# A two-layer hybrid trunk in split fp32: the first output projection in pairs by seven products, and changes at the start, in the last pair and in the final norm

## The chip, the cores and the metric

One core of one Trainium2 chip. The metric is the device time of one execution in microseconds, the median over the runs. Engines are named as in the profile: PE (TensorE), DVE (VectorE), ACT (ScalarE), POOL (GpSimd), SP (SyncE, which here only issues transfers).

## The reference

Two layers act on x, which has 512 tokens of 1024 channels, all in float32. Each layer does this:

```python
h = rmsnorm(x, norm_g[layer])
u = h @ w_in[layer]                       # q, k, v, z of three mixers, and merge gates ga, gb, gc
...
merged = (sigmoid(ga) * (ya @ w_br_a[layer]) + sigmoid(gb) * (yb @ w_br_b[layer])
          + sigmoid(gc) * (yc @ w_br_c[layer]))
x = x + merged @ w_out[layer]
```

ya is forgetting attention (4 heads), yb a dilated mixture (6 heads), yc sliding-window attention with sinks (6 query heads on 2 key heads), each times a SiLU gate. A final RMSNorm of x follows the second layer.

## The kernel before

All activations are held transposed: a tile has 128 channels on the partitions and the 512 tokens as its free size, so x is 8 such tiles, k = 0 to 7. PE's fast fp32 format keeps only part of a number, so every operand is split in a high half (fp32r) and a low half (the rest), and every product is made of three matmuls: high times high, high times low, low times high (mm3, L128 to L132). The half sums go to one bank of PSUM. Weights come in chunks of 128 x 512: wh is the high half, wl the low half. For most weights POOL issues the load of wh, ACT writes the negated high half to wl (L1146), and POOL issues a second load that accumulates the weights on top (L1147): wl is then the low half, without work of DVE. For the weights that load raw (layer 0's V, and the last projection, "plain") ACT casts the high half (L1140) and DVE or POOL subtracts (L1142).

A list of items, built once, sets the order of the work: each has a PE function with the weight chunks it takes, or is an evacuation without chunks. A loop at the end walks through it (from L1180 on): ahead of a step it loads and splits what that step takes, behind it loads up to RINGH = 10 chunks ahead and splits up to RING = 7 ahead. The order written so is then refined by the compiler's scheduler, except in a stretch that is put under a manual schedule, where it stays as written.

Per layer: the V projection (v_item L225: for each k, four token blocks of three 512-column matmuls, in four "att" banks that collect over k), attention, the mixers' gate projections, and the merge of 8 output rows M0 to M7. Six of the merge's steps are pairs (pair_steps L646): two rows' gate products are worked out by seven products of half size instead of eight, from sums and differences of quarters of the weights and of x (forms 0 to 6; the sums of x are made once by sums L598, in four places SH and SL: vb, PH and PL, P). The pair's results of 256 columns are combined by DVE from banks a, b and c (c11, c12, c22, c21), with ACT's help, and each row is then normed, gated and merged (norm, gate, merge). merge writes the high half MH by ACT and the low half ML by DVE; M6 and M7 come from the last pair (2, 6).

Behind layer 0's merge stands the first output projection (o_item L778): 8 outputs e, each of 24 matmuls of 512 columns over the 8 merged rows. DVE adds the residual (L789), the sum goes out to x1d, ACT and DVE split it into XH and XL of the second layer (split_x L149), and its square is summed by ACT and POOL (square_sum L162). Between the outputs stand the second layer's V items.

Behind layer 1's merge stands the last projection (last_item, last_projection L861): 16 steps of 24 matmuls of 256 columns, first the first half of the tokens for the 8 outputs, then the second half. From the last pair of layer 1 on a manual schedule holds. DVE adds the residual (L828), ACT squares (L834, L837) and scales (L842), DVE sums the squares (L839). The final norm takes the column sums by PE (rms_pe, L176), a root by ACT and DVE (rms_root), a transpose of the reciprocal to a row on all partitions (rbc_pe, L217), a copy of it by ACT (L848) and the products (store_half, L856 on POOL, L858 on DVE).

The start: g goes out on ACT's queue (L106), the tiles of x and V's first weights in turn on SP's; ten matmuls of zeros (L1156) keep PE busy until the first V item.

## Time and profile before

| what | value |
| --- | --- |
| median of 3 runs | 881.96 us (880.96 to 884.07) |
| profiled execution, its time | 880.83 us |
| its span in the profile | 879.1 us |
| mean granted clock of PE | 0.995 |
| busy: PE, DVE, ACT, POOL | 864.6, 569.0, 510.8, 441.9 us |
| moved by DMA | 163.83 MB |

The span is the time from the first to the last instruction that the profile holds; the execution's own time is somewhat longer. Busy times of engines overlap. In a row of the timeline the first number is the start from the span's beginning, the second the duration, both in us, then engine, line, operation, what it writes and reads, shapes and how many are grouped; in brackets the idle time ahead of it and what ended that. Matmuls are pipelined, so their durations overlap and the time that each takes is the distance from start to start.

### The profile page before, as it was taken

Reading aid. Unit: us, or ns where it says so; the run is one execution under the profiler, and the core shown is the slowest. Engines: PE = TensorE matmul, PEld = TensorE weight load, DVE = VectorE, ACT = ScalarE, POOL = GpSimd, SP = SyncE. Lnnn points to the kernel's source line nnn. Section 1 sums busy time; section 2 is a strip of 40 time slices with the busy share of each in tenths; the row PEclk is TensorE's granted clock in tenths of the full one; section 3 lists DMA queues with packets and bytes.
Section 4 is the critical chain, followed back from the end, with each engine's and each line's share of the span. In section 5 each row is a group of like instructions: output and inputs, shape, how many; then the busy total and the mean of one; then the engine's idle time right before and its main releaser. Section 6 shows DMA issues by size and latency. Waiting matters only on the chain.

```text
span 879.1 us, 14412 instructions
## 1 busy us (share of the span) xinstructions
PE 864.6 (98%) x4866; PEld 750.8 (85%) x4866; DVE 569.0 (65%) x1250; ACT 510.8 (58%) x1076; POOL 441.9 (50%) x570
## 2 busy tenths in 40 slices
PE   9999999999999999999999999999999999999995
PEld 6988888888888899997889888888888888999994
DVE  7546688577676768762123658876685867687643
ACT  7377566575656655554335856666465765556552
POOL 5354576665444254566664546667544444544211
PEclk9999999999999999999999999999999999999998
DMA  8697777978989899999997887788799897998423
GB/s 293 142 212 146 152 151 166 184 149 180 196 188 235 205 181 249 206 192 288 255 240 151 173 167 153 146 168 172 157 205 199 181 249 162 206 250 189 133 71 113
DMA packets 97082, 163.83 MB, mean 186 GB/s; under 512 B 12144, under 2 KB 26864, under 8 KB 97008
## 3 DMA queue, kind: packets, MB, share of 16 engines
q0 software_dynamic: 71424, 121.70, 68.9%
q1 hardware_dynamic: 25440, 41.20, 14.2%
q8 instruction: 38, 0.62, 0.3%
q14 instruction: 36, 0.29, 0.1%
q10 hardware_dynamic: 144, 0.01, 0.0%
HBM read 153.43 MB, written 4.19 MB: 179 GB/s over the span
## 4 chain that ended last, share of the span: by engine, by line
PE 75%; issue 8%; POOL 6%; DMA 6%; DVE 3%; ACT 1%; SPq 0%; POOLq 0%; DVEq 0%; ACTq 0%
PE mm L130 16%; PE mm L131 16%; PE mm L132 16%; PE att L130 4%; PE att L131 3%; PE att L132 3%; PE pv L549 3%; POOL wl L1147 3%; POOL wh L1117 3%; PE att L503 3%; PE att L439 2%; PE att L438 2%; DMA tmp<-in_xT_dram 2%; PE att L234 1%; PE att L235 1%
## 5 line engine op out<-in xcount | busy, mean ns | idle before, releaser
L1147 POOL DMA_DIRECT2D wl<-in_wpk_dram x248 | 224.0, 921 | 179.4 <-ACT wl L1146 147.9
L1117 POOL DMA_DIRECT2D wh<-in_wpk_dram x248 | 168.8, 685 | 176.1 <-PE mm L132 129.4
L1146 ACT ACTIVATE wl<-wh 128x512 fp32r<-128x512 f32 (+3 forms) x248 | 147.9, 601 | 139.8 <-PE mm L132 107.5
L130 PE MATMUL mm<-xh,wh 128*128 128x512 f32 x544 | 217.7, 400 | 0.0
L131 PE MATMUL mm<-xl,wh 128*128 128x512 f32 x544 | 214.6, 394 | 0.0
L132 PE MATMUL mm<-xh,wl 128*128 128x512 f32 x544 | 214.4, 394 | 0.0
L132 PEld LDWEIGHTS mm<-xh,wl 128*128 128x128 f32 x544 | 102.2, 188 | 24.0
L130 PEld LDWEIGHTS mm<-xh,wh 128*128 128x128 f32 x544 | 102.4, 188 | 22.1
L131 PEld LDWEIGHTS mm<-xl,wh 128*128 128x128 f32 x544 | 102.4, 188 | 22.0
L474 ACT ACTIVATE P<-P,ng 128x256 f32<-128x256 f32 (+3 forms) x128 | 67.0, 525 | 24.6 <-DVE ng L472 24.1
L529 DVE TENSOR_TENSOR PL<-att,PH 128x512 fp32r<-128x512 f32 (+2 forms) x84 | 46.1, 599 | 7.0 <-ACT PH L528 7.0
L130 PE MATMUL mm<-y,wh 128*128 128x512 f32 (+1 forms) x132 | 49.9, 378 | 0.2 <-ACT y L711 0.2
L131 PE MATMUL mm<-y,wh 128*128 128x512 f32 (+1 forms) x132 | 49.9, 378 | 0.0
L132 PE MATMUL mm<-y,wl 128*128 128x512 f32 (+1 forms) x124 | 47.5, 383 | 0.0
L130 PE MATMUL att<-xh,wh 128*128 128x256 f32 x144 | 40.6, 282 | 1.3 <-DVE tmp L740 1.3
L132 PE MATMUL att<-xh,wl 128*128 128x256 f32 x144 | 40.4, 281 | 0.0
L131 PE MATMUL att<-xl,wh 128*128 128x256 f32 x144 | 40.4, 281 | 0.0
L492 DVE TENSOR_SCALAR P<-P,den 128x256 f32<-128x256 f32 (+3 forms) x128 | 39.7, 376 | 1.0
L528 ACT CAST PH<-att 128x512 fp32r<-128x512 f32 (+2 forms) x84 | 38.7, 526 | 1.3 <-PE att L503 0.6
L439 PE MATMUL att<-qk,qk 128*128 128x256 f32 (+2 forms) x128 | 37.0, 308 | 0.0
L503 PE MATMUL att<-ident,P 128*128 128x128 f32 x284 | 36.2, 272 | 0.0
L438 PE MATMUL att<-qk,qk 128*128 128x256 f32 (+2 forms) x128 | 36.1, 308 | 0.0
(260 smaller groups left out, 2039.4 us busy)
## 6 DMA issues: line engine op xcount, KB each, us to landing
wh<-in_wpk_dram POOLq DMA_DIRECT2D x196, 256.0 KB, 4.6
wl<-in_wpk_dram POOLq DMA_DIRECT2D x196, 256.0 KB, 5.1
y<-in_wpk_dram SPq DMA_DIRECT2D x32, 256.0 KB, 5.4
qk<-in_wpk_dram SPq DMA_DIRECT2D x24, 256.0 KB, 5.3
wh<-in_wpk_dram POOLq DMA_DIRECT2D x32, 192.0 KB, 4.7
wl<-in_wpk_dram POOLq DMA_DIRECT2D x32, 192.0 KB, 4.5
tmp<-tmp SPq DMA_DIRECT2D x80, 64.0 KB, 3.8
mg<-in_xT_dram SPq DMA_DIRECT2D x8, 256.0 KB, 6.6
```

The lines of the kernel that those rows point to most:

```text
L130: nc.tensor.matmul(ps, wh, xh, start=first, stop=False, skip_group_check=part)
L131: nc.tensor.matmul(ps, wh, xl, start=False, stop=False, skip_group_check=part)
L132: nc.tensor.matmul(ps, wl, xh, start=False, stop=last, skip_group_check=part)
L438: nc.tensor.matmul(ps, q[:, qs], kh[:, a:a + n], start=True, stop=False)
L439: nc.tensor.matmul(ps, q2[:, qs], k2[:, a:a + n], start=False, stop=True)
L474: nc.scalar.activation(pb, pb, AF.Exp, bias=ng[:, i:i + 1], scale=-1.0, accum_out=den[:, i:i + 1])
L492: nc.vector.tensor_scalar(blks[i], blks[i], den[:, i:i + 1], None, op0=ALU.mult)
L503: nc.tensor.transpose(ps[:, c * P:(c + 1) * P], pt[:, src * P:(src + 1) * P], st["ident"])
L529: nc.vector.tensor_tensor(st["PL"][:, o:o + n], bk[:, :n], rd(hh), op=ALU.subtract)
L1117: nc.gpsimd.dma_start(hl[i][0][:, :w], ap)
L1146: nc.scalar.activation(lo[:, :w], rd(h[:, :w]), AF.Copy, scale=-1.0)
L1147: nc.gpsimd.dma_start(lo[:, :w], ap, accum_op=ALU.add)
```

## The change

It has four parts.

1. *First loads.* g goes out first on SP, V's first weights on ACT's queue, and ACT's table load stands behind it. There are 7 warm-up matmuls in place of 10.
2. *First output projection.* Outputs 0 and 1 stay as they are. Outputs (2, 3), (4, 5), (6, 7) are pairs by seven products of 12 matmuls with 256 columns (o_pair). Their sums of x are now sums of the merged rows (four_sums, for k = 0 to 3), in the same places as before. The pairs' weights load raw by SP's queue, 4 quarters of 256 KB each, and are cast by ACT and subtracted by DVE (L1217 differences, L1238 casts, L1240 low halves). The squares are summed by DVE. The order is output 0, 1, pair (2, 3), V0, V1, pair (4, 5), V2, V3, pair (6, 7), V4 to V7. V's low halves stand in the tiles va0 to va3, which are empty then, and take no place of the seven of wl.
3. *Last pair of layer 1 and last projection.* Weights are loaded and split one step later, behind the evacuations of the step. Of the low halves of the last projection's first chunks, four stay on POOL and four go to DVE.
4. *Final norm.* The column sums begin with a matmul of zeros and then take all of the accumulator's columns, the last squares last. The reciprocal row of the second half is written to two banks, one for DVE and one for ACT.

```diff
-    nc.scalar.dma_start(g_sb, gT)
+    nc.sync.dma_start(g_sb, gT)
...
-            eng = nc.vector if k == KT - 1 else nc.gpsimd
+            eng = nc.vector if k == KT - 1 else side
...
-        for n, tb in enumerate(tbs):
-            for j, a in enumerate(accs):
-                nc.tensor.matmul(ps[:, tb:tb + 1], st[a][:, n * P:(n + 1) * P], ones,
-                                 start=j == 0, stop=j == len(accs) - 1)
+        zero = st["PH"]
+        c = slice(tbs[0], tbs[-1] + 1)
+        nc.tensor.matmul(ps[:, c], zero[:, :P], zero[:, :len(tbs)], start=True, stop=False)
+        for j, a in enumerate(accs):
+            for n, tb in enumerate(tbs):
+                nc.tensor.matmul(ps[:, tb:tb + 1], st[a][:, n * P:(n + 1) * P], ones, start=False,
+                                 stop=j == len(accs) - 1 and n == len(tbs) - 1)
...
+    def four_sums(k, a, b):
+        u, v = tmp(), tmp()
+        nc.vector.tensor_tensor(u[:, T0], a[:, T1], b[:, T1], op=ALU.add)
+        nc.vector.tensor_tensor(u[:, T1], u[:, T0], a[:, T0], op=ALU.subtract)
+        nc.vector.tensor_tensor(v[:, T0], a[:, T0], a[:, T1], op=ALU.subtract)
+        nc.vector.tensor_tensor(v[:, T1], b[:, T0], u[:, T1], op=ALU.subtract)
+        h, lo = sum_places(k)
+        for n, w in ((0, u), (1, v)):
+            c = slice(n * S, n * S + S)
+            nc.scalar.copy(h[:, c], w)
+            nc.vector.tensor_tensor(lo[:, c], w, rd(h[:, c]), op=ALU.subtract)
+        st["SH", k], st["SL", k] = h, lo
...
+    def o_pair(l, e, bank, res, finish):
...
+        def add(u, tok, b, first):
+            def run():
+                if u not in x:
+                    x[u] = tmp()
+                other = st["xr", e + u] if first else x[u]
+                nc.vector.tensor_tensor(x[u][:, tok], d[b], other[:, tok], op=ALU.add)
+                if not first:
+                    finish(e + u, x[u], tok)
+            return urgent(run)
+
+        res(e)
+        prod("a", 0, M(0, T0))
+        do(add(0, T0, "a", True))
+        prod("c", 1, M(1, T0))
+        do(add(0, T0, "c", False))
+        prod("b", 2, sum_part(1))
+        do(add(1, T1, "b", True))
+        prod("a", 3, sum_part(2))
+        do(add(1, T0, "a", True))
+        prod("b", 4, sum_part(4))
+        do(add(1, T0, "b", False))
+        prod("a", 5, sum_part(3))
+        do(add(1, T1, "a", False), add(0, T1, "a", True))
+        prod("e", 6, M(1, T1))
+        do(add(0, T1, "e", False))
...
-            o_item(0)
-            for e in range(1, 8):
-                o_item(e)
-                v_item(1, e - 1)
-            v_item(1, 7)
+            first_projection()
...
+    def first_projection():
...
+        do(lambda: load_res(0), lambda: load_res(1), sums_m(0))
+        o_item(0)
+        do(sums_m(1))
+        o_item(1)
+        do(sums_m(2), sums_m(3))
+        o_pair(0, 2, mm_bank, res, finish)
+        v_item(1, 0)
+        v_item(1, 1)
+        o_pair(0, 4, mm_bank, res, finish)
+        v_item(1, 2)
+        v_item(1, 3)
+        o_pair(0, 6, mm_bank, res, finish)
+        for k in range(4, 8):
+            v_item(1, k)
...
-                eng = nc.gpsimd if key[:2] == LAST_O and key[3] == 0 else nc.vector
+                eng = nc.gpsimd if key[:2] == LAST_O and key[3] == 0 and key[2] > 3 else nc.vector
...
-    for _ in range(10):
+    for _ in range(7):
...
-                    nc.sync.dma_start(t[:, :w], ap)
+                    (nc.scalar if i == 0 else nc.sync).dma_start(t[:, :w], ap)
...
+        if key[:2] == ("v", 1):
+            return h, T([P, S], F32R, f"va{key[2] % 4}")
...
+            if key[:2] != ("v", 1):
+                if since is not None and sum(j >= since for j in ring) >= RING:
+                    return
+                ring.append(i)
...
-        nc.scalar.copy(rbc, st["rb"][:, :HT])
+        nc.scalar.copy(rbc, st[f"rb{hf}"][:, :HT])
...
         step(lambda _: rbc_pe(_, h1))
+        step(lambda _: rbc_pe(_, h1, "rb1", att_bank))
         do(lambda: store_half(1))
...
+        if later is not None:
+            load(later + RINGH)
+            split_to(later + RING)
+            later = None
...
-        load(pos + RINGH if n > 4 else pos + 8)
-        split_to(pos + RING)
+        if "late" in st:
+            later = pos
+        else:
+            load(pos + RINGH if n > 4 else pos + 8)
+            split_to(pos + RINGH, pos)
```

How the order of the instructions moves, at two places. The first is DVE in the first output projection, behind the evacuation of the output before. Before, for outputs 0 to 2 (tmp is the sum, xl its low half):

```order
L789 TENSOR_TENSOR tmp_4451<-mm_4421,sz_4417 128x512
L159 SCALAR_TENSOR_TENSOR xl_883_4457<-tmp_4451,g_61,xh_882_4456 128x512
L789 TENSOR_TENSOR tmp_4497<-mm_4462,sz_4419 128x512
L159 SCALAR_TENSOR_TENSOR xl_893_4503<-tmp_4497,g_61,xh_892_4502 128x512
L789 TENSOR_TENSOR tmp_4565<-mm_4535,sz_4453 128x512
L159 SCALAR_TENSOR_TENSOR xl_909_4571<-tmp_4565,g_61,xh_908_4570 128x512
```

After, around output 1's addition (L803; wl are weights' low halves, L610 to L613 the four sums of merged rows, PL their low halves):

```order
L1240 TENSOR_TENSOR wl_4518<-xh_862_4319,wh_4408 128x512
L803 TENSOR_TENSOR tmp_4521<-mm_4485,sz_4420 128x512
L1240 TENSOR_TENSOR wl_4582<-xl_861_4317,wh_4459 128x512
L1240 TENSOR_TENSOR wl_4586<-xl_863_4321,wh_4510 128x512
L159 SCALAR_TENSOR_TENSOR xl_904_4525<-tmp_4521,g_61,xh_903_4524 128x512
L170 TENSOR_TENSOR ys_4471<-ys_4471,tmp_4528 128x512
L610 TENSOR_TENSOR tmp_4531<-mg_2025,mg_2698 128x256
L612 TENSOR_TENSOR tmp_4532<-mg_2025 128x256
L611 TENSOR_TENSOR tmp_4531<-tmp_4531,mg_2025 128x256
L610 TENSOR_TENSOR tmp_4541<-mg_2345,mg_2981 128x256
L613 TENSOR_TENSOR tmp_4532<-mg_2698,tmp_4531 128x256
```

Where two additions and splits of x followed each other, weight splits, the sum of squares and the sums of the merged rows now stand between them; wl_4586 is the low half of form 6 of pair (2, 3).

The second place is ACT, at the end of the last pair of layer 1 and the start of the last projection. Before (L692 the gate, L711 the high half of a merged row, L1140 weight casts, L834 and L837 squares, L842 scaling):

```order
L692 ACTIVATE tmp_8811<-tmp_8811 128x256
L711 CAST y_1744_8894<-mg_7262 128x256
L1140 CAST wh_8933<-xl_1749_8931 128x512
L834 ACTIVATE ys_9032<-mg_9028 128x256
L842 ACTIVATE mg_9028<-mg_9028,gf_294 128x256
L1140 CAST wh_8952<-xl_1753_8950 128x512
L1140 CAST wh_8981<-xh_1759_8979 128x512
L837 ACTIVATE tmp_9074<-mg_9070 128x256
```

After (L709, L728, L1238, L915, L918 and L923 are the same steps):

```order
L709 ACTIVATE tmp_9041<-tmp_9041 128x256
L728 CAST y_1791_9125<-mg_7499 128x256
L1238 CAST wh_9152<-xl_1796_9150 128x512
L915 ACTIVATE ys_9262<-mg_9258 128x256
L923 ACTIVATE mg_9258<-mg_9258,gf_291 128x256
L1238 CAST wh_9173<-xl_1799_9171 128x512
L918 ACTIVATE tmp_9301<-mg_9297 128x256
L923 ACTIVATE mg_9297<-mg_9297,gf_291 128x256
```

The cast ahead of the first square was that of output 3's first chunk (wh_8933) and is now that of output 2's second (wh_9152): output 3's first chunk (wh_9173) stands behind the first square and scaling, its second behind the next ones. And DVE there, after (L763 is c21, L716 and L717 the merge, L729 the low half of a merged row, L909 the additions of the residual):

```order
L1240 TENSOR_TENSOR wl_9201<-xl_1793_9129,wh_9131 128x512
L763 TENSOR_TENSOR tmp_9041<-att_9026,rbc_5356 128x256
L716 SCALAR_TENSOR_TENSOR tmp_9041<-tmp_9041,mm_9112 128x256
L717 TENSOR_TENSOR mg_7499<-mg_7499,tmp_9041 128x256
L729 TENSOR_TENSOR y_1792_9126<-mg_7499,y_1791_9125 128x256
L1240 TENSOR_TENSOR wl_9226<-xl_1796_9150,wh_9152 128x512
L909 TENSOR_TENSOR mg_9258<-mm_9233,sz_9229 128x256
L1240 TENSOR_TENSOR wl_9269<-xl_1799_9171,wh_9173 128x512
L909 TENSOR_TENSOR mg_9297<-mm_9272,sz_9231 128x256
```

wl_9201 and wl_9226 are output 2's low halves: the first was POOL's, the second stood ahead of c21; now the second stands behind the merge.

## Rows read from the trace of the kernel before

**Rows 1.** The page, busy time of the PE engine, share of the span, instructions.

```profile
PE 864.6 (98%) x4866; PEld 750.8 (85%) x4866; DVE 569.0 (65%) x1250; ACT 510.8 (58%) x1076; POOL 441.9 (50%) x570
```

**Rows 2.** What PE waited for: us in total, times, the longest.

```profile
PE att L130 <- DVE tmp L740: 1.3, 1, 1.3
PE pv L176 <- ACT tmp L837: 0.8, 1, 0.8
```

**Rows 3.** Timeline of PE, the start.

```profile
1.51 4.63 PE L1156 MATMUL pv<-qk 128*128 128x512 f32 x10 [1.51 <-DVE qk L1153]
5.94 1.46 PE L233 MATMUL att<-wh,xh 128*128 128x512 f32 x3
```

**Rows 4.** Timeline of ACT, the start.

```profile
4.39 0.91 ACT L156 ACTIVATE xh<-mg,g 128x256 fp32r<-128x256 f32 x2 [1.70 <-DMA g<-in_gT_dram]
```

**Rows 5.** Timeline of PE, last pair of layer 0 and output 0.

```profile
376.22 0.28 PE L130 MATMUL att<-xh,wh 128*128 128x256 f32 x1
...
379.77 0.28 PE L130 MATMUL att<-vb,wh 128*128 128x256 f32 x1
...
391.01 0.39 PE L130 MATMUL mm<-qk,wh 128*128 128x512 f32 x1
...
395.63 0.40 PE L132 MATMUL mm<-y,wl 128*128 128x512 f32 x1
396.19 0.50 PE L130 MATMUL mm<-y,wh 128*128 128x512 f32 x1 [0.16 <-ACT y L711]
```

**Rows 6.** Busy time by stretch, first projection: PE, PEld, DVE, ACT, POOL (instructions), clock, DMA.

```profile
391.00:458.00 67.00, 66.84 (x289) 53.74 (x288) 15.00 (x25) 26.98 (x45) 44.23 (x58) 1.00 1.10 260
```

**Rows 7.** Timeline of DVE, three operations in a row.

```profile
805.18 0.43 DVE L746 TENSOR_TENSOR tmp<-att,rbc 128x256 f32<-128x256 f32 x1
805.52 0.68 DVE L1142 TENSOR_TENSOR wl<-y,wh 128x512 fp32r<-128x512 f32 x1
806.12 0.68 DVE L712 TENSOR_TENSOR qk<-mg,qk 128x512 fp32r<-128x512 f32 x1
```

**Rows 8.** The page, DMA issues: count, size, median us from issue to landing.

```profile
wl<-in_wpk_dram POOLq DMA_DIRECT2D x196, 256.0 KB, 5.1
```

**Rows 9.** The same from the DMA view of 391 to 458 us.

```profile
wl<-in_wpk_dram POOLq DMA_DIRECT2D x22, 256.0 KB, 6.7
```

**Rows 10.** Timeline of PE, form 6 of the last pair; output 3's first matmul.

```profile
819.07 0.39 PE L130 MATMUL att<-xh,wh 128*128 128x256 f32 x1 [1.28 <-DVE tmp L740]
...
829.11 0.29 PE L130 MATMUL mm<-qk,wh 128*128 128x256 f32 x1
```

**Rows 11.** Timeline of DVE, last pair and output 0 of the last projection.

```profile
815.65 1.34 DVE L686 TENSOR_TENSOR tmp<-tmp,rbc 128x256 f32<-128x256 f32 x1
...
823.87 0.69 DVE L1142 TENSOR_TENSOR wl<-xl,wh 128x512 fp32r<-128x512 f32 x1
824.48 0.42 DVE L746 TENSOR_TENSOR tmp<-att,rbc 128x256 f32<-128x256 f32 x1
825.38 0.42 DVE L699 SCALAR_TENSOR_TENSOR tmp<-tmp,mm 128x256 f32<-128x256 f32 x1 [0.48 <-ACT tmp L692]
...
826.73 0.43 DVE L712 TENSOR_TENSOR y<-mg,y 128x256 fp32r<-128x256 f32 x1 [0.47 <-ACT y L711]
827.08 0.42 DVE L828 TENSOR_TENSOR mg<-mm,sz 128x256 f32<-128x256 f32 x1
```

**Rows 12.** Timeline of ACT, the cast ahead of the first square.

```profile
826.61 0.61 ACT L1140 CAST wh<-xl 128x512 fp32r<-128x512 f32 x1
```

**Rows 13.** Timeline of all engines, the final norm of the second half.

```profile
868.04 0.38 PE L176 MATMUL pv<-ones,tmp 128*128 128x1 f32 x2 [0.85 <-ACT tmp L837]
...
870.17 0.40 PE L217 MATMUL pv<-ident,r 128*128 128x128 f32 x2 [1.30 <-DVE r L207]
870.66 0.37 ACT L848 COPY rbc<-pv 128x256 f32<-128x256 f32 x1 [1.49 <-PE pv L217]
871.07 2.08 DVE L858 TENSOR_TENSOR tmp<-pv,mg 128x256 f32<-128x256 f32 x6 [1.05 <-ACT rbc L848]
```

More of the change, by code (lines that the diff above doesn't have):

```diff
@@ L601, in run, with sums_m, part, sum_part @@
                 nc.scalar.activation(t, t, AF.Copy, scale=g_sb[:, l, kk:kk + 1])
-            u, v = tmp(), tmp()
-            nc.vector.tensor_tensor(u[:, T0], a[:, T1], b[:, T1], op=ALU.add)
-            nc.vector.tensor_tensor(u[:, T1], u[:, T0], a[:, T0], op=ALU.subtract)
-            nc.vector.tensor_tensor(v[:, T0], a[:, T0], a[:, T1], op=ALU.subtract)
-            nc.vector.tensor_tensor(v[:, T1], b[:, T0], u[:, T1], op=ALU.subtract)
-            h, lo = sum_places(k)
-            for n, w in ((0, u), (1, v)):
-                c = slice(n * S, n * S + S)
-                nc.scalar.copy(h[:, c], w)
-                nc.vector.tensor_tensor(lo[:, c], w, rd(h[:, c]), op=ALU.subtract)
-            st["SH", k], st["SL", k] = h, lo
-        return run
+            four_sums(k, a, b)
+        return run
+    def four_sums(k, a, b):
[10 more added lines that the diff above has]
+        st["SH", k], st["SL", k] = h, lo
+    def sums_m(k):
+        return lambda: four_sums(k, st["M", k], st["M", k + 4])
+    def part(hs, ls, half, tok):
+        return lambda k: (hs[k + 4 * half][:, tok], ls[k + 4 * half][:, tok])
+    def sum_part(m):
+        c = slice((m - 1) * HT, m * HT)
+        return lambda k: (st["SH", k][:, c], st["SL", k][:, c])
+    def products(key, d, new_bank):
+        def prod(bank, form, xf):
+            def pe(HL):
+                new = bank not in d
+                if new:
+                    d[bank] = (pv_bank if bank == "e" else new_bank)()[:, :HT]
+                wh, wl = HL[0]
+                for k in range(4):
+                    c = slice(k * P, (k + 1) * P)
+                    xh, xl = xf(k)
+                    mm3(d[bank], wh[:, c], wl[:, c], xh, xl, new and k == 0, k == 3, bank not in "ce")
+            step(pe, [key + (form,)])
+        return prod
     def m_item(l, br, i):
@@ L651, in pair_steps @@
         now = urgent
+        prod = products(("w", l, br, i), d, att_bank)
         def A(half, tok):
-            return lambda k: (XH[k + 4 * half][:, tok], XL[k + 4 * half][:, tok])
-        def Sm(m):
-            c = slice((m - 1) * HT, m * HT)
-            return lambda k: (st["SH", k][:, c], st["SL", k][:, c])
-        def prod(bank, form, xf):
-            def pe(HL):
-                new = bank not in d
-                if new:
-                    d[bank] = att_bank()[:, :HT]
-                wh, wl = HL[0]
-                for k in range(4):
-                    c = slice(k * P, (k + 1) * P)
-                    xh, xl = xf(k)
-                    mm3(d[bank], wh[:, c], wl[:, c], xh, xl, new and k == 0, k == 3,
-                        bank != "c")
-            step(pe, [("w", l, br, i, form)])
+            return part(XH, XL, half, tok)
         def branch(u):
@@ L1050, in tile_trunk, with is_split @@
     LAST_O = ("o", L - 1)
-    PAIRS = [k[2:4] for k in seq if k[0] == "w" and k[1] == 0 and k[4] == 0]
+    SUMS = (2, 3, 5, 6)
+    def is_split(key):
+        return is_plain(key) or key[0] == "w" and (key[4] in SUMS or key[2] == 3)
     def is_plain(key):
@@ L1127, in source, with split_to @@
         return o
-    def split_to(n):
+    ring = []
+    def split_to(n, since=None):
         while ptr["split"] < min(n, ptr["load"]):
@@ L1148, in split_to @@
             ptr["split"] += 1
-    warm = T([P, 1], F32, "warm")
-    nc.scalar.activation(warm, ones, AF.Exp)
     cold = T([P, S], F32R, "qk", 12)
@@ L1159, in tile_trunk @@
         load(min(k + 1, 5))
+        if k == 0:
+            nc.scalar.activation(T([P, 1], F32, "warm"), ones, AF.Exp)
     split_x(xs[0], 0, 0, 2)
```

61 lines of the change are left out of this document (42 added, 19 removed).

## The prediction

> **What bounds the kernel now.** I read the busy shares first, then what TensorE (PE) waited for, then stretches of the timeline. PE is busy 864.6 of 879.1 us [rows 1], and the two largest waits that the change touches are 1.3 and 0.8 us [rows 2]. So time goes only in three ways: fewer matmul columns, one of these waits, or the head and tail of the program where PE isn't full. A new wait of PE adds to the time one for one. The sum stands against the profiled execution, 880.83 us, which lies 1.1 us below the median of the runs, 881.96; I carry the difference over to the median.
>
> **The start.** The vector g goes out first on SP, V's first weights go out on ACT's queue, and there are 7 warm-up matmuls in place of 10. Now ten warm-ups take 4.63 us, and the first real matmul starts at 5.94 [rows 3]; its XH0 waited for g until 4.39 [rows 4]. With three warm-ups less (3 x 0.46 = 1.4 us) PE is free at 4.7. V0's cast now stands ahead of x0's low halves on DVE, so XH0 sets the start: its first half is 0.45 us of ACT (half of 0.91 [rows 4]), and if g lands no later than now the first matmul can follow from 4.9 on. I expect some 5.2, so -0.7 us, between -1.3 (the whole of the warm-ups) and +1.6. The upper end is the clock: the warm-ups at 0.46 us each and the first three real matmuls at 1.46/3 = 0.49 [rows 3] run at the lower level of 1.2 GHz, while a 512-column matmul later takes 0.23 us [rows 5]. PE was busy from 1.51 on before the clock rose; if an idle gap of half a microsecond ahead of the real matmuls made the rise come late, so that ten more of these ran at the lower level, they would cost 10 x 0.23 = 2.3, less 0.7: +1.6. The Trainium skill's page "TensorE: Matmul & The Clock Gate", in Part 1, says that the throttled state is the default and that activity releases it, which speaks against fewer warm-ups; by it alone this term would be +1.6 rather than -0.7. I take -0.7, since both PE's first busy stretch and the real matmuls behind it count as activity, with a gap that is small beside either.
>
> **First-layer projection, matmuls.** Six outputs of 24 matmuls with 512 columns become three pairs of 7 x 12 with 256. The paces are start to start: 30 matmuls from 376.22 to 379.77 give 0.118 us for 256 columns, 20 from 391.01 to 395.63 give 0.231 for 512 [rows 5]. 144 x 0.231 = 33.3 against 252 x 0.118 = 29.7: -3.6 us. Output 0 also stood still for some 0.55 us at 395.9 to 396.6, where the merged row 6 came late (next start 396.19 where 395.86 was due, and that matmul lasts 0.50) [rows 5]; ACT copies fewer low halves there now, and I count -0.5 (0 to -0.6).
>
> **First-layer projection, VectorE.** DVE does 15 us of work in the 67 us of this stretch [rows 6], and now gets nearly all of it. Between output 0's addition and the last weight split of pair (6,7) stand, by the order, 40 operations of 512 columns, 6 low halves of x and 30 of 256 columns. Start to start an independent one takes 0.60 and 0.34 us, alone 0.68 and 0.43 [rows 7]; at 0.61, 0.68 and 0.38 that is 24.4 + 4.1 + 11.4 = 40 us, at the full durations 45, and PE's own work in between is 45 as well (output 1, V0 to V3, the pairs but for their last product: 24 x 0.231 + 48 x 0.231 + 240 x 0.118). So DVE keeps up on the mean, with nothing to spare, and is late where the order bunches its work: ahead of and in pair (2,3), where the four sums of rows 2 and 3 of the merge (12 operations), five weight splits and output 1's evacuation stand in one row. Counting that queue down from output 0's end at 397, form 6's low half is done at 406.3 where PE wants it at 405.9, and the third row's sums are ready at 409.3 and 410.4, each behind PE: 0.35 + 0.45 + 0.3 = +1.1 us. All this is nothing if DVE goes through at 0.34 for the short ones, and 3.5 at the full durations.
>
> **V's low halves.** They are still made by ACT and an accumulating transfer. ACT's step for V1 stands behind x1's scaling, which waits for DVE (406.3), that for V3 behind the cast of pair (4,5)'s form 6, which waits for DVE's subtraction (427.8). With 5.1 us from issue to landing, the median over the program [rows 8], V1 is 0.4 late and V3 1.7: +2.1 us. This stretch itself shows 6.7 us [rows 9], under 23 such transfers and as many first loads; 12 of either go away, so I stay near the first. At 4.7 the two would cost 1.3, at 6.7 they cost 5.1. The projection in all: -3.6 - 0.5 + 1.1 + 2.1 = -0.9 us, between -4.2 and +3.
>
> What POOL loses (12 first loads, 12 accumulating ones, six additions) costs nothing by itself: no row of PE waits for POOL here. SP's 12 raw loads go out behind loads that are long due; if they came late, form 0 of a pair would show it.
>
> **The last pair and the last projection.** Weight splits now follow a step's evacuations, and four low halves move from POOL to DVE. What goes: PE waited 1.3 us for form 6 until 819.07 [rows 10], because an evacuation ahead of it took 1.34 us instead of 0.42 (815.65 [rows 11]) beside POOL's low half; counted down, form 6 starts at 818.4: -0.7. What comes: DVE now has output 1's and 2's low halves, 0.69 each, in front of and between the merges. Each merge goes DVE, DVE, ACT, DVE, about 1.8 us with its round trip (825.38 to 827.16 [rows 11]). The evacuation c21 stays at about 824.5, where it is now [rows 11], its merge ends at 827.3, and output 2's second low half, which was done at 824.56 [rows 11], now stands behind it: ready at 828.1, while PE, now 0.7 early, wants it at 827.2. Output 0's evacuation waits behind that split (828.0 in place of 827.08 [rows 11]), then its square and scaling on ACT, and only then ACT casts output 3's halves: 829.4 and 832.0, where the first was cast at 826.61, ahead of output 0's evacuation [rows 12]. Their low halves are ready at 830.7 and 833.3; output 3, which began at 829.11 [rows 10], now ends 2.6 us later than before. Stalls of 1.0, 1.2 and 1.1, less 0.7: +2.6 us. From output 4 on the queue has caught up. The bounds: -1.3 if nothing is late, +3.5 if the round trips take a tenth longer.
>
> **The final norm.** The accumulator's matmuls go ahead, so after the last square two remain where four stood (from 868.04 [rows 13], the pairs 0.23 apart): -0.2. Now ACT copies the reciprocal row from 870.66, and DVE's products start at 871.07, after 1.05 us idle, once that copy has ended [rows 13]. With a bank for each DVE starts behind the first transposes, two more of which ACT waits for (0.40 us for two [rows 13]): -0.4. -0.6 us, between -0.8 and 0.
>
> **Sum:** -0.7 - 0.9 + 2.6 - 0.6 = +0.4 us on 880.83; on the median 881.96 + 0.4, rounded, 882.4 us. One measurement of this kernel tells a change from none beyond about 0.3%, 2.65 us: no change runs from 879.3 to 884.6.
>
> **The rivals.**
> 1. *The last pair isn't late.* If DVE's chain of merges runs some 1.5 us ahead of my count, output 3's halves are cast in time and only the gone wait is left: 882.4 - 2.6 - 1.3 = 878.5. For it: the queue catches up within one output. Against it: the order puts the casts behind the squares whatever the durations. Chance 0.15.
> 2. *DVE keeps ahead in the pairs.* With short operations at 0.34 and transfers at 4.7 us only 0.3 us and 1.3 us of waits are left: 882.4 - 1.6 = 880.8; together with half of rival 1, 878.8, faster. Chance 0.10.
> 3. *Slower: the accumulating transfers stay at 6.7 us.* Place: V1 and V3 of the second layer's V, whose low halves start only after DVE's queue lets ACT go. Price: 5.1 in place of 2.1 us, so 885.4. It decides from about 6.3 us on. For it: this stretch's own rows [rows 9]. Against it: half of the software transfers go. Chance 0.16.
> 4. *Slower: the clock comes late*, by 1.6 in place of -0.7: 882.4 + 2.3 = 884.7. Chance 0.05.
> 5. *The pairs don't do what they say*: if the shorter matmuls waited at each change of bank or operand, 252 x 0.118 would not hold; at 0.13 the matmuls save 0.5 and the time is 885.5. Forms of the same shape in the rows run at 0.118 [rows 5], so 0.03.
>
> **How the numbers follow.** My forecast case holds 0.51. Faster comes from rivals 1 and 2: 0.25. Slower from 3, 4 and 5: 0.24. Same: 0.51. The range takes in rivals 1 and 3 and stops there: 878.2 to 885.8; the ends of several terms at once lie outside.
>
> **What would show it.** Right: PE waits for DVE at form 6 and at the sums of pair (2,3), and for a transfer ahead of V3; in the last projection PE waits at outputs 2 and 3, with DVE's first evacuation at 828 relative to the same place; no wait of PE for form 6 in the last pair; DVE's last products start with ACT's copy, not after it. Wrong: no wait of PE between the eighth and the last output, a DVE busy share below 70% in the pairs, or slow matmuls past the first five at the start.

## The result, and the profile after

The changed kernel takes 887.0 us (median of 7 runs, 884.09 to 889.56); the kernel before took 880.2 us beside it (7 runs, 879.82 to 884.07). The ratio is 1.0066, with a 95% interval of 1.0053 to 1.0078: **slower by 5.8 us** (4.7 to 6.9), where +0.4 was forecast and the range ended at 885.8. (The medians lie 6.8 us apart, the means 5.7.) The profiled execution took 887.0 us, with a span of 885.2 (before 879.1) and a mean granted clock of 0.997.

The page shows that the work moved as the order said. PE is as busy as before [rows 1] in a longer span, so the loss is waiting:

```profile
PE 865.4 (98%) x4977; PEld 753.2 (85%) x4977; DVE 606.1 (68%) x1335; ACT 519.6 (59%) x1093; POOL 413.7 (47%) x536
```

What PE waited for in the changed kernel: us in total, times, the longest. Some rows are left out.

```profile
PE mm L264 <- DMA wl<-in_wpk_dram: 2.4, 2, 1.3
...
PE att L237 <- DMA va<-in_wpk_dram: 1.4, 1, 1.4
...
PE att L130 <- DVE tmp L757: 1.2, 2, 1.0
...
PE mm L130 <- ACT wh L1238: 0.8, 2, 0.4
PE mm L132 <- DMA wl<-in_wpk_dram: 0.7, 1, 0.7
```

Before, form 6 was the longest of these [rows 2]. Now the longest is L264: the matmuls of the second layer's item f, which makes the forgetting attention's V and its forget gate (four chunks of 520 columns). They stand *behind* the changed stretch. Where the loss arose is read from the starts of the same matmul in both timelines of PE. The head of a last pair is the start of form 6 of the pair ahead of it, from which PE runs through to the last pair's form 3:

| matmul | before | after | difference |
| --- | --- | --- | --- |
| first real one | 5.94 | 5.04 | -0.9 |
| layer 0, head of the last pair | 375.5 | 376.0 | +0.5 |
| layer 0, last pair, form 6 | 389.6 | 391.5 | +1.9 |
| second layer's norm, column sums | 458.40 | 459.08 | +0.7 |
| the same norm, transposes (f stands between) | 470.78 | 474.68 | +3.9 |
| layer 1, head of the last pair | 803.6 | 808.6 | +5.0 |
| layer 1, last pair, form 6 | 819.1 | 823.8 | +4.7 |
| final norm, first half's sums | 848.87 | 856.88 | +8.0 |
| final norm, second half's transposes | 870.17 | 878.11 | +7.9 |
| end of the span | 879.1 | 885.2 | +6.1 |

So the start and the projection gained (-0.9, and -1.2 from 391 to 459), and three places lost: +1.4 at the end of layer 0's last pair, +3.2 at f, +3.0 in the last projection. The +1.4 from the first matmul to 375 and the +1.1 between 475 and 808 lie where the change touches next to nothing; over the same two stretches the runs below, whatever their edits, show -1.0 to +2.8 and 0.0 to +1.5. The tail behind the transposes took 7.1 us, against 8.9 before (last section).

**The place at f.** POOL's timeline over the projection (start, duration, line, operation; in brackets its idle time and what ended it):

```profile
424.95 0.85 POOL L1245 DMA_DIRECT2D va<-in_wpk_dram  x1 [8.34 <-ACT va L1244]
425.50 0.86 POOL L1206 DMA_DIRECT2D wh<-in_wpk_dram  x1
430.76 0.84 POOL L1245 DMA_DIRECT2D va<-in_wpk_dram  x1 [4.39 <-ACT va L1244]
438.44 0.52 POOL L366 MEMSET qk<- 64x512 f32 x1 [6.84 <-PE mm L131]
438.96 2.68 POOL L1206 DMA_DIRECT2D wh<-in_wpk_dram  x5
...
456.38 0.88 POOL L1245 DMA_DIRECT2D wl<-in_wpk_dram  x1 [4.45 <-ACT wl L1244]
457.55 4.36 POOL L1245 DMA_DIRECT2D wl<-in_wpk_dram  x5 [0.30 <-ACT wl L1244]
```

POOL is little busy here, but it takes its instructions in order. L366, a memset of the second layer's q2 that the change doesn't touch, now stands ahead of V4's first load and waits 6.84 us for a tile that PE still reads. The five loads behind it go out in a burst from 438.96 on, and the ones behind these, from 447.44 on, land only 7.9 to 9.2 us after issue. Among them are f's, and the six accumulating transfers of wl follow from 456.38. Before, the same memset stood between loads and waited for nothing (first row: POOL, the kernel before):

```profile
449.61 0.52 POOL L363 MEMSET qk<- 64x512 f32 x1
```

And PE, in the changed kernel, at the second of its two waits at f:

```profile
461.63 0.28 PE L263 MATMUL mm<-wh,xh 128*128 128x260 f32 x1
463.03 0.39 PE L264 MATMUL mm<-wl,xh 128*128 128x260 f32 x1 [1.11 <-DMA wl<-in_wpk_dram]
```

**The place at 388.** SP, POOL, ACT and PE of the changed kernel, from their timelines:

```profile
378.57 0.33 SPq L1201 DMA_DIRECT2D xl<-in_wpk_dram  x1
379.00 0.86 SPq L1201 DMA_DIRECT2D xh<-in_wpk_dram  x2
379.90 0.42 SPq L1201 DMA_DIRECT2D xl<-in_wpk_dram  x1
...
387.00 0.63 ACT L1244 ACTIVATE wl<-wh 128x512 fp32r<-128x512 f32 x1 [2.88 <-DMA wh<-in_wpk_dram]
...
387.93 0.86 POOL L1245 DMA_DIRECT2D wl<-in_wpk_dram  x1 [3.97 <-ACT wl L1244]
...
389.40 0.50 PE L132 MATMUL mm<-y,wl 128*128 128x512 f32 x1 [0.74 <-DMA wl<-in_wpk_dram]
```

Pair (2, 3)'s four raw loads leave from 378.57 on, as soon as the last pair's form 0 has read the tiles that they fill. From 376 to 392 POOL's first loads of 256 KB now take 8.4 us to land (median of three), where they took 6.3 before (of eight), and PE waits behind the matmul at 388.26 for a low half.

### The profile page after: what moved, and what is told of

Read it like the earlier page. It is cut to its first block, busy times and chain, and to the rows that moved or that the text cites. A ratio compares the mean times of both kernels' runs of the same rounds, so it can differ in the third digit from the quotient of the medians.

```text
span 885.2 us, 14720 instructions
## 1 busy us (share of the span) xinstructions
PE 865.4 (98%) x4977; PEld 753.2 (85%) x4977; DVE 606.1 (68%) x1335; ACT 519.6 (59%) x1093; POOL 413.7 (47%) x536
## 4 chain that ended last, share of the span: by engine, by line
PE 77%; DMA 7%; issue 7%; DVE 4%; ACT 2%; SPq 1%; POOL 1%; POOLq 0%; DVEq 0%; ACTq 0%
PE mm L132 17%; PE mm L130 17%; PE mm L131 17%; PE att L130 4%; PE att L131 4%; PE att L132 4%; PE pv L552 4%; PE att L506 3%; PE att L442 2%; PE att L441 2%; DMA wh<-in_wpk_dram 2%; DMA tmp<-tmp 1%; DMA va<-in_wpk_dram 1%; SPq L351 1%; DMA wl<-in_wpk_dram 1%
## 5 line engine op out<-in xcount | busy, mean ns | idle before, releaser
L1245 POOL DMA_DIRECT2D wl<-in_wpk_dram x228 | 207.7, 935 | 192.6 <-ACT wl L1244 158.0
L1206 POOL DMA_DIRECT2D wh<-in_wpk_dram x236 | 162.8, 719 | 152.3 <-PE mm L132 111.1
L1244 ACT ACTIVATE wl<-wh 128x512 fp32r<-128x512 f32 (+3 forms) x228 | 135.1, 598 | 103.9 <-PE mm L132 77.7
L130 PE MATMUL mm<-y,wh 128*128 128x512 f32 (+1 forms) x126 | 46.7, 371 | 0.0
L131 PE MATMUL mm<-y,wh 128*128 128x512 f32 (+1 forms) x126 | 46.7, 370 | 0.0
L132 PE MATMUL mm<-y,wl 128*128 128x512 f32 (+1 forms) x118 | 44.6, 378 | 0.7 <-DMA wl<-in_wpk_dram 0.7
L442 PE MATMUL att<-qk,qk 128*128 128x256 f32 (+2 forms) x128 | 37.1, 309 | 0.5 <-DVE qk L378 0.5
L356 DVE TENSOR_TENSOR tmp<-tmp,sin 128x512 f32<-128x512 f32 x20 | 13.8, 690 | 34.6 <-DMA tmp<-tmp 34.6
```

Of the source, the lines that this page charges most:

```text
L130: nc.tensor.matmul(ps, wh, xh, start=first, stop=False, skip_group_check=part)
L131: nc.tensor.matmul(ps, wh, xl, start=False, stop=False, skip_group_check=part)
L132: nc.tensor.matmul(ps, wl, xh, start=False, stop=last, skip_group_check=part)
L442: nc.tensor.matmul(ps, q2[:, qs], k2[:, a:a + n], start=False, stop=True)
L1206: nc.gpsimd.dma_start(hl[i][0][:, :w], ap)
L1244: nc.scalar.activation(lo[:, :w], rd(h[:, :w]), AF.Copy, scale=-1.0)
```

## The experiments

Four kernels take one part of the change each; the others repair one suspected loss. Offsets are starts of the same matmuls, each run's profile minus the kernel before's, in us; "last pair" is the head of layer 1's, and "last projection's end" is read at the final norm's first column sums, ten of its 16 steps in. Single profiles scatter by 1 us and more in the parts of the program that no edit touches, so a step from column to column says more than a column. The ratio is over all runs, the offsets come from one of them: e11's profile is of the slowest of its twelve runs (885.47 us, median 882.02), part3_last's of the fastest of ten (882.03, median 883.52).

| run | form 6, layer 0 | norm 2, sums | norm 2, transp. | last pair | its form 6 | last projection's end | time ratio (95%) |
| --- | --- | --- | --- | --- | --- | --- | --- |
| the change | +1.9 | +0.7 | +3.9 | +5.0 | +4.7 | +8.0 | 1.0066 (1.0053 to 1.0078) |
| part1_start | 0.0 | +0.3 | +0.3 | +1.5 | +1.5 | +1.6 | 0.9993 (0.998 to 1.0006) |
| part2_pairs | +1.1 | -0.3 | +4.1 | +5.3 | +5.3 | +5.3 | 1.0022 (1.0007 to 1.0037) |
| part3_last | -1.0 | -1.5 | -1.5 | -1.5 | -2.0 | +1.2 | 1.0026 (1.0012 to 1.0039) |
| part4_norm | +0.1 | +0.8 | +0.9 | +0.9 | +0.9 | +0.9 | 0.9999 (0.9987 to 1.0011) |
| e5_no_pool_memset | +1.0 | +0.2 | +0.4 | +1.0 | +0.7 | +4.0 | 1.0037 (1.0019 to 1.0055) |
| e6_raw_loads_late | +0.8 | -0.6 | +2.2 | +3.0 | +2.7 | +6.0 | 1.0076 (1.0053 to 1.0099) |
| e7_late_only | -0.4 | 0.0 | 0.0 | 0.0 | -1.4 | +0.1 | 1.0000 (0.9991 to 1.0009) |
| e8_dve_halves_only | 0.0 | +0.8 | +0.8 | +0.8 | +0.2 | +0.9 | 1.0011 (0.9999 to 1.0023) |
| e9_raw_rows_6_7 | -0.6 | +6.1 | +9.2 | +9.6 | +9.1 | +12.5 | 1.0112 (1.0094 to 1.0131) |
| e10_halves_on_pool | +0.3 | -0.7 | +2.1 | +2.4 | +1.0 | +2.8 | 1.0034 (1.0019 to 1.0048) |
| e11_halves_pool_no_memset | +2.6 | +2.1 | +3.8 | +5.3 | +3.9 | +5.7 | 1.0005 (0.9993 to 1.0018) |
| e12_three_repairs | -1.0 | +7.2 | +8.4 | +8.7 | +7.3 | +8.9 | 1.0057 (1.0038 to 1.0076) |
| e13_no_pairs | -0.1 | -0.2 | -0.1 | +0.1 | -1.3 | +0.3 | 1.0001 (0.9988 to 1.0013) |
| e14_two_raw_loads_late | -0.5 | +1.8 | +3.3 | +4.3 | +2.9 | +4.7 | 1.0040 (1.0022 to 1.0058) |

**part1_start: the kernel before with part 1 alone.**

```diff
-    nc.scalar.dma_start(g_sb, gT)
+    nc.sync.dma_start(g_sb, gT)
...
-    for _ in range(10):
+    for _ in range(7):
```

> The kernel before with the first loads and 7 warm-ups alone. Theory (the loss of the whole change comes from the pairs' transfers and from the last pair): the first real matmul starts near 5.0 and all later work 0.7 us earlier, time -0.5 to -1 us against before. Rival (a late clock at the start): +1 us or more, with matmuls at 0.43 us or more past the fifth.

The first real matmul starts 0.8 us earlier, and the ratio of 0.9993 agrees with -0.7 us without telling it from nothing.

**part2_pairs: the change without parts 1, 3 and 4** (their hunks undone; `o_pair` and what belongs to it stays).

> The kernel before with the pairs of the first projection alone (with V's low halves in va0 to va3). Theory: the products save 3.6 us but PE waits for weights' transfers ahead of the stretch, inside it for V3, and behind it for the f weights, 3.9 us later at the second layer's transposes than 0.7 earlier at the first's; time +3.5 to +5 us. Rival (the loss is in the last pair alone): -0.5 to -1.5 us.

Slower by 1.9 us, less than the 3.5 to 5 expected, as the end of the program came 1.7 us sooner than the theory had it (last section). From form 6 to the sums of norm 2 it gains 1.4, but the steps ahead (+1.7, from -0.5 at the last pair's head) and behind (+4.4 at f, part of it the clock, last section) are there without any other part.

**part3_last: the kernel before with part 3 alone.**

```diff
+        if "late" in st:
+            later = pos
...
-                eng = nc.gpsimd if key[:2] == LAST_O and key[3] == 0 else nc.vector
+                eng = nc.gpsimd if key[:2] == LAST_O and key[3] == 0 and key[2] > 3 else nc.vector
```

> The kernel before with weights split one step later in the last pair and four low halves moved to DVE, alone. Theory: PE waits for form 6 and then at outputs 1 to 3 for casts and low halves, together some 2.5 to 3.3 us more than before; time +2.5 to +3.3 us. Rival (only late because the change arrives there later and out of step): within 1 us of before, no wait at outputs 2 and 3.

From the last pair's head to the projection's end: from -1.5 to +1.2, a loss of 2.6 us, as the prediction's +2.6. The time agrees: 1.0026 is 2.3 us.

**part4_norm: the kernel before with part 4 alone.**

> The kernel before with the final norm's order of sums and second bank alone. Theory: -0.6 us (0.2 from the sums, 0.4 from DVE no longer behind ACT's copy). Rival, from the profile of the whole change, where the stretch from the transposes to the end of the span was 1.8 us shorter: -2 us.

From the transposes to the first store's issue pass 1.22 us instead of 1.68, and the time doesn't show it; why is told in the last section.

**e5_no_pool_memset: the changed kernel; DVE writes q2's 1/32 instead of POOL.**

```diff
-                nc.gpsimd.memset(rd(q2[b, :]), 1.0 / 32)
+                nc.vector.tensor_scalar(q2[b, :], t[b, :], 0.0, 1.0 / 32, op0=ALU.mult, op1=ALU.add)
```

> The changed kernel with the second layer's q2 halves (1/32 in 64 rows) written by DVE out of the row it has just made, in place of POOL's memset, which in the changed kernel stands for 6.8 us at the head of POOL's queue, behind it the first loads of V4 to V7 and of the f weights. Theory (POOL's queue in order delays the f weights): V4 to V7's first loads go out near 431.5 in place of 438.9, PE no longer waits for the f weights' low halves (2.7 us lost there), and the time falls by 2.5 to 3.5 us against the changed kernel, to about 884 by its median of 887. Rival (the loads wait for places of wh that pair (6,7) still holds, or for the DMA engines): the loads go out no earlier and the time stays within 1 us.

The step at f falls from +3.2 to +0.2, and no wait of PE is left there. POOL's timeline of this run, where the memset stood:

```profile
429.98 0.88 POOL L1206 DMA_DIRECT2D wh<-in_wpk_dram  x1
432.77 0.54 POOL L1206 DMA_DIRECT2D wh<-in_wpk_dram  x1 [1.91 <-PE att L238]
...
440.57 0.53 POOL L1206 DMA_DIRECT2D wh<-in_wpk_dram  x1 [0.90 <-PE mm L132]
```

V4's first load leaves at 429.98 and the next ones as their tiles come free, instead of five together at 438.96. The ratio falls by 0.0029 (2.6 us); the two intervals just overlap, so it is the profile that settles this. The same edit stands in e11, e12 and e14, where the step at f is 1.7, 1.2 and 1.5; the five profiles with the pairs and the memset on POOL show 2.8 to 4.4. So the memset is most of the loss at f, not all of it.

**e6_raw_loads_late: the changed kernel; the first pair's raw loads written behind the last pair's form 6.**

```diff
-                return [f"xh{e}", f"xl{e}", f"xh{e + 1}", f"xl{e + 1}"], ("w", 0, 2, 6, 0 if e == 2 else 6)
+                return [f"xh{e}", f"xl{e}", f"xh{e + 1}", f"xl{e + 1}"], ("w", 0, 2, 6, 6)
```

> The changed kernel with the raw loads of pair (2,3) let out once the last pair's form 6 has its weights, not its form 0: some 13 us later. Theory (these four loads of 256 KB delay the last pair's and output 0's weights on the DMA engines): PE's waits at 388 and 391 us (0.9 + 0.4 lost) go, time -1.3 us against the changed kernel, unless form 0 or 1 of pair (2,3) now waits. Rival (the low half there is late for ACT's or POOL's sake): the waits stay.

Inconclusive: SP still issues the four loads at 377.49, as the scheduler puts a load where its tile comes free, not where it is written. PE waits 0.7 us at the same place, and the ratio stays.

**e7_late_only and e8_dve_halves_only: the kernel before with one half of part 3 each** (e7 the first hunk shown under part3_last, e8 the second).

> The kernel before with weights split one step later in the last pair, all eight low halves still on POOL. Theory (the order, which puts output 3's casts behind the squares, makes the waits): the waits for casts at outputs 2 and 3 stay, time +1.5 to +2.5 us against before. Rival (DVE's four additional low halves make them): no wait at outputs 2 and 3, time within 0.7 us.

> The kernel before with four of the last projection's low halves on DVE in place of POOL, in the old order. Theory: form 6's wait shrinks by 0.7 to 0.9 us since POOL no longer slows DVE there, and output 1 to 3 wait little, time -0.7 to +0.5 us. Rival: DVE becomes late by two low halves, 1.4 us, time +0.7 us or more.

Neither loses what both lose, and the theory of e7 fell. The late splits alone start form 6 1.4 us earlier and give 1.5 back; the halves on DVE alone cost 0.1 in the profile, and their ratio, 1.0011, isn't clear of 1. PE's waits from 800 to 850 us, with late splits alone:

```profile
PE mm L132 <- POOL wl L1142: 0.8, 1, 0.8
PE mm L130 <- ACT wh L1140: 0.2, 1, 0.2
```

and with both (part3_last):

```profile
PE mm L130 <- ACT wh L1140: 0.8, 2, 0.4
PE att L130 <- DVE tmp L740: 0.5, 1, 0.5
PE mm L132 <- DVE wl L1142: 0.4, 2, 0.2
PE mm L132 <- DVE va L1142: 0.2, 1, 0.2
PE mm L130 <- DVE tmp L699: 0.2, 1, 0.2
```

With both, the splits come behind the evacuations *and* four of them stand in DVE's queue; PE then waits in turn for a cast, a low half, a cast. With the halves on POOL waits of 0.8 and 0.2 are left.

**e9_raw_rows_6_7: the changed kernel; the first pair's raw loads in tiles that come free only at form 6's end.**

```diff
-                e = key[3]
-                return [f"xh{e}", f"xl{e}", f"xh{e + 1}", f"xl{e + 1}"], ("w", 0, 2, 6, 0 if e == 2 else 6)
+                e = 4 if key[3] == 4 else 6
+                return [f"xh{e}", f"xl{e}", f"xh{e + 1}", f"xl{e + 1}"], ("w", 0, 2, 6, 6)
```

> The changed kernel, with the first projection pair's four raw loads in the tiles of rows 6 and 7 (free only after the last form of the layer-0 last pair) instead of rows 2 and 3 (free two forms after its start); the third pair uses the same tiles again. Theory 1: in the changed kernel these loads go out on SP at 378.6 and crowd the first loads of the weights, which made PE wait for a low half at 388 and form 6 start 1.9 us later than before (0.5 before the wait). Then form 6 starts at +0.5, and the run is about 1.4 us shorter than the changed kernel: ratio to the kernel before 1.0050 in place of 1.0066. Theory 2: the low half is late because of what stands ahead of it in POOL's and ACT's queues; form 6 stays at +1.5 to +2 and the ratio at 1.0066. Either way, if the raw loads now leave only at 392, they land at 398 or later, and the first product of pair (2,3), wanted at about 402 behind a cast and a subtraction, may come 1 to 3 us late; then the ratio is higher by that much.

Both halves of the expectation held. With the loads at 389.46 and later the wait at 388 is gone: form 6 keeps the offset of the last pair's head, -0.6. But the pair's products wait; PE's waits from 395 to 470 us:

```profile
PE att L237 <- DMA va<-in_wpk_dram: 2.8, 3, 1.0
PE mm L130 <- ACT wh L1238: 2.0, 2, 1.8
PE mm L132 <- DVE wl L1240: 1.0, 1, 1.0
```

From form 6 to norm 2's sums this run loses 6.6 us where the change gains 1.2, far more than the 1 to 3 expected: the lateness goes on to V's low halves, and the clock fell as well (last section).

**e10_halves_on_pool: the changed kernel; all low halves of the last projection's first chunks on POOL** (part3_last's second hunk undone).

> The changed kernel with the low halves of outputs 0 to 3 of the last projection back on POOL (weight splits behind the evacuations kept). Theory 1: the last pair's 3 us (from the plateau of its forms at +5.0 to the last projection's end at +8.0) come only from both parts of the change together: splits behind the evacuations, and four more low halves in DVE's queue. Then the offset at the end of the last projection stands at about +5.1, and the time at about 884.1: ratio 1.0033 in place of 1.0066. Rival: the late splits alone make ACT's casts late once the first layer is changed as well; the ratio stays above 1.0055.

From the last pair's head to the projection's end now +0.4 instead of +3.0; ratio 1.0034, expected 1.0033.

**e11_halves_pool_no_memset: e5's and e10's edits together.**

> The changed kernel with both repairs: q2's 1/32 written on VectorE instead of by POOL's memset, and the last projection's low halves back on POOL. Theory: the two losses lie at different places of the program and add: 2.6 (measured, 1.0066 to 1.0037) and 2.9 (expected of the halves) of 5.8 us, so about 881.2, ratio 1.0004, and PE waits for no weight at f's matmuls nor for a cast in the last projection. Rival: each repair only uncovers the next late resource, and the two together save under 4 us: ratio above 1.0020.

1.0005 against 1.0004: the two losses add, and with both repaired the change costs nothing that can be measured. The offsets of its profile, up to +5.7, don't say otherwise: they are of its slowest run, which stood at +1.8 at the head of layer 0's last pair already, where only the start differs. One detail missed: 1.0 us of waits at f is left in this profile, and one cast is late by 0.4.

**e12_three_repairs: e5's, e9's and e10's edits together.**

> All three repairs: raw loads in the tiles of rows 6 and 7, no memset on POOL, low halves on POOL. If each removes its loss (1.4, 2.6, 2.9 of 5.8 us), the time is 1.1 us under the kernel before: ratio 0.9988, and the pairs pay for themselves. Rival: late raw loads cost at pair (2,3) what they save at 388; then it is no better than the kernel with two repairs, 1.0004 or up to 1.003.

The rival, and worse: the late raw loads cost 4.6 us over e11 (0.0052), much as e9's 4.1 over the change (0.0046). In both profiles the clock fell (last section), so not all of it is waiting.

**e13_no_pairs: the kernel before with part 1, e7's late splits and part 4; no pairs.**

> The kernel before with the new start, the new norm and the weight splits behind the evacuations; no pairs in the first projection, all eight low halves of the last one on POOL. By the single parts (ratios 0.9993, 0.9999, 1.0000) the sum is 0.9992, 881.3 on a before of 882. Theory 1: the pairs with their repairs pay nothing, because what the columns save (1.2 us in the stretch) goes to the waits at 388, V3 and f; then this kernel is as fast as or faster than the changed one with two repairs (1.0005), by up to 0.0013. Theory 2: the repaired pairs pay 1 us; then this one is above 1.0005.

1.0001 against e11's 1.0005. The pairs with their repairs pay nothing that can be measured, for or against.

**e14_two_raw_loads_late: e11, with two of the first pair's four raw loads in row 6's tiles.**

```diff
+                return {2: ["xh2", "xl2", "xh6", "xl6"], 4: ["xh4", "xl4", "xh5", "xl5"],
+                        6: ["xh7", "xl7", "xh6", "xl6"]}[e], ("w", 0, 2, 6, 0 if e == 2 else 6)
```

> The changed kernel with two repairs (no memset on POOL, low halves on POOL), and only two of the first projection pair's four raw loads in the early tiles (rows 2); the other two go to row 6's tiles and leave after the last pair's form 6. Theory 1: the wait at 388 goes with the crowd, and the two late loads are wanted only at the pair's second form, so it is not late: 1.0 to 1.4 us less than the kernel with two repairs, ratio 0.999 to 0.9993. Rival: half the crowd still makes the low half late by as much, or the late two make the pair's first sums wait by 1 to 3 us: ratio 1.0005 to 1.004.

The wait at 388 is gone here too (form 6 at -0.5, as the last pair's head), but the time is 1.0040. PE waits from 395 to 470 us:

```profile
PE att L237 <- DMA va<-in_wpk_dram: 2.7, 2, 1.5
PE mm L130 <- ACT y L728: 1.4, 1, 1.4
```

A second one of V's low halves, at 413, and output 0's merged row are late now; the change waited for neither. No version was found that beats the kernel before.

## Why the prediction was wrong

**The start: right.** -0.7 was forecast for a first matmul at 5.2; it came at 5.04, -0.9. How much of this lasts to the end isn't shown: at the head of layer 0's last pair the ten profiles with this start lie 0.1 us ahead of the kernel before on the mean, the five with the old start 0.4. Rival 4 fell: one matmul took half a microsecond, then they stood 0.23 apart (the latest of the ten, e10's, has 0.43 to 0.59 for the first five). The rule weighed there would have made it +1.6; this trace doesn't bear it out. PE's timeline:

```profile
5.04 0.66 PE L236 MATMUL att<-wh,xh 128*128 128x512 f32 x1 [0.17 <-ACT xh L156]
5.53 0.39 PE L237 MATMUL att<-wl,xh 128*128 128x512 f32 x1
5.76 0.39 PE L238 MATMUL att<-wh,xl 128*128 128x512 f32 x1
```

**The projection itself: right in sum, -0.9 forecast and -1.2 measured** between form 6 and norm 2's sums. DVE's queue was full, as counted; busy times by stretch in the columns of [rows 6]:

```profile
391.00:438.00 47.00, 45.33 (x279) 39.25 (x278) 45.92 (x94) 26.36 (x49) 6.50 (x9) 1.00 0.62 159
```

DVE is busy 45.92 of 47 us, and PE lost 0.9 us in pair (2, 3), where 1.1 was forecast: eight steps of 0.24 or less beyond its pace, from 407.20 to 412.41, too short to stand among the waits above. Some of V0's matmuls run between the pair's there, which the count from the order didn't have. V3 waited where it should, and lost 1.5 us for 1.7 (ACT and PE):

```profile
429.83 0.63 ACT L1244 ACTIVATE va<-wh 128x512 fp32r<-128x512 f32 x1 [0.78 <-DMA wh<-in_wpk_dram]
...
433.50 0.39 PE L236 MATMUL att<-wh,xh 128*128 128x512 f32 x1
435.25 0.51 PE L237 MATMUL att<-va,xh 128*128 128x512 f32 x1 [1.37 <-DMA va<-in_wpk_dram]
```

V1's 0.4 came to 0.1. Rival 3 fell where it was placed: V's accumulating transfers took 4.6 us, under the 5.1 taken. But V3's cause is another than the forecast's, and its size is luck: ACT was through with pair (4, 5)'s casts and waited 0.78 us for V3's first load. That load left POOL at 425.50, behind V2's accumulating transfer, which had held the queue for 8.34 us.

**The step that failed** is the one that set POOL and SP at nothing: "What POOL loses (12 first loads, 12 accumulating ones, six additions) costs nothing by itself: no row of PE waits for POOL here", and the sentence on SP's raw loads behind it. Fewer instructions of POOL are no guarantee of earlier loads. With its work thinned out, what is left in its in-order queue waits for others: V's accumulating transfers for ACT, then a memset for PE, and every later load stands behind. That is e5's 2.6 us. SP's raw loads were not late, as the prediction asked; they were early, and made POOL's loads late: form 6's +1.4 (0.6 to 1.7 in the six profiles that leave these loads early), gone in e9, e12 and e14. The Trainium skill's page "DMA: Bandwidth & Descriptors", section "SWDGE vs HWDGE vs iDMA", says that POOL's transfers and those of SP feed different queues inside each DMA engine, which serves them in turn; the trace fits this, with 8.4 us to landing instead of 6.3, but doesn't show the turns. Both costs lie outside the stretch from 391 to 458 that I counted, one behind it and one ahead. The criterion was wrong as well: in these views a late load of POOL is a wait for DMA, never for POOL.

**The last pair and projection: right, +2.6 forecast, +3.0 measured** (+2.6 with part 3 alone). PE lost 1.0 us in output 2 and 1.1 us in each half of output 3, where 1.0, 1.2 and 1.1 were forecast. In detail, the wait for form 6 went only in part: 0.97 us is left, against 1.28 [rows 10]. Output 3's halves are cast behind output 0's and 1's squares, as counted: ACT, the changed kernel:

```profile
833.80 0.42 ACT L915 ACTIVATE ys<-mg 128x256 f32<-128x256 f32 x1 [1.09 <-DVE mg L909]
834.67 0.60 ACT L1238 CAST wh<-xl 128x512 fp32r<-128x512 f32 x1
...
837.23 0.60 ACT L1238 CAST wh<-xl 128x512 fp32r<-128x512 f32 x1
```

At the last pair's offset of +5.0 the forecast 829.4 and 832.0 stand for 834.4 and 837.0. What the prediction missed is that neither half of the part does this alone (e7, e8).

**The final norm: right for DVE, wrong for the end.** DVE's products start 0.44 us behind the transposes instead of 0.90 [rows 13], without waiting for ACT's copy, and the last squares' part took 0.23 less. But the -0.6 reaches nothing that ends the program: POOL's two products still wait for ACT's copy, which the change makes later, and the span ends behind them (last section):

```profile
878.11 0.40 PE L220 MATMUL pv<-ident,r 128*128 128x128 f32 x2 [1.30 <-DVE r L210]
...
878.82 0.37 ACT L929 COPY rbc<-att 128x256 f32<-128x256 f32 x1 [1.71 <-PE att L220]
...
878.55 2.08 DVE L939 TENSOR_TENSOR tmp<-pv,mg 128x256 f32<-128x256 f32 x6 [0.59 <-PE pv L220]
```

**The sum.** The forecast's +0.4 lacked +1.4 at 388 and +3.2 at f in the profile; with them it is +5.0, inside the measured 4.7 to 6.9. That this fits is in part luck. The profile's +6.1 also holds +2.5 in the two stretches that the change hardly touches, 0 in place of the norm's -0.6, and -2.0 behind POOL's last product, which the prediction didn't have. The ratios of the four parts multiply to 1.0040, 2.3 us short of the whole, which their intervals can't tell from nothing. Rivals 1 and 2 fell; rival 5 too, as the projection gained. Two sums in the prediction are slightly off and change nothing: DVE's work at the full durations is 44 us, and V1 and V3 at 6.7 us cost 5.3.

**Open.** Why f keeps 1.0 us of waits in e11, where the memset is gone, isn't settled. No run takes V3's wait away by itself. How much of the 388 wait reaches the time alone is known from profiles only, as both ways to remove it cost more elsewhere.

## What to carry to other kernels

When work leaves an in-order queue, list what stays in it and what each of these now waits for, to the end of the program: an operation that was harmless between busy neighbours (here a memset) can come to the front and hold every load behind it. Count a change's transfers over the stretches before and after the one it rewrites, since a load that leaves as soon as its tile is free competes with loads that are due sooner, and one that is moved later may itself be late. Two edits that are harmless alone, later splits and four more of them on the same engine, may cost what neither does, so they should be measured alone and together.

## What the runs showed that was not expected

**The clock fell after two waits close together.** In part2_pairs PE waited 0.90 and 1.29 us at f, the second until 464.10. Busy times by stretch; PEclk is the third number from the end:

```profile
460.00:464.00 4.00, 1.90 (x13) 1.48 (x12) 2.98 (x10) 2.42 (x4) 3.02 (x5) 1.00 1.02 172
464.00:466.00 2.00, 1.90 (x9) 1.90 (x10) 1.03 (x3) 0.19 (x1) 0.00 (x0) 0.54 1.12 204
466.00:468.00 2.00, 2.00 (x12) 2.00 (x12) 0.00 (x0) 0.28 (x1) 0.00 (x0) 0.60 1.20 335
```

The granted clock went to the lower level of 1.2 GHz for most of 464 to 468, and matmuls of 260 columns stood 0.22 us apart instead of 0.12. In the changed kernel's profile PE waited there about as long (2.4 us) and the clock stayed at 1.00. In e9 it fell as well, to 0.50 from 408 to 414, in the second of two gaps of 1.95 and 1.21 us beyond PE's pace, and in e12 from 409 to 415. So a wait can cost more than its length, not in every run. The change's two slowest runs, 888.37 and 889.56 us, have the lowest mean clocks of its seven, 0.992 and 0.993 (the others 0.994 to 0.997); where in them the clock fell isn't recorded.

**The program's end follows POOL, and came sooner with the pairs.** POOL's last products, first in the kernel before, then in the changed one:

```profile
871.11 1.41 POOL L856 TENSOR_TENSOR tmp<-mg,rbc 128x256 f32<-128x256 f32 x2 [12.28 <-ACT rbc L848]
```

```profile
879.27 1.41 POOL L937 TENSOR_TENSOR tmp<-mg,rbc 128x256 f32<-128x256 f32 x2 [12.32 <-ACT rbc L929]
```

From their end to the span's end pass 6.5 us in each of the seven kernels without the pairs, and 4.5 to 4.9 us in each of the nine with them. That is why the tail shrank from 8.9 to 7.1 us. The pairs' kernels have 24 transfers of POOL fewer, 472 for 496; whether this is the reason wasn't tested. So the pairs were paid 1.7 to 2.0 us here that the prediction, which put what POOL loses at nothing, didn't count either. The norm was paid nothing: in part4_norm the transposes come 0.25 us sooner behind the second half's sums, and POOL's products end 0.22 us later behind the transposes. What DVE and the stores gain there, 0.46 us, ends nothing.
